# Rotating banks in the first Strassen pairs, copies on ScalarE, spread conditioning rows, and a first norm split between GpSimd and ScalarE

## The chip, the cores and the metric

The kernel runs on one NeuronCore of a Trainium2 chip, as one program with one launch. The metric is the device time of one execution in microseconds, as the median of several runs. Where a time is read inside the program it comes from one profiled execution, which has its own device time and its own span from the first to the last instruction.

## The reference, cut to what matters

One encoder layer is computed for 576 tokens: 64 frames of a running stream (group 1) and 512 frames of a new one (group 0). The matmuls keep fp32 accuracy.

```python
mod = silu(c) @ w_ada + b_ada              # 6 rows of 1024 per group: shift, scale, gate, twice
h   = rmsnorm(x, norm1_g) * (1 + sc1) + sh1
q, k, v, glu_in, g = split(h @ w_in)       # one input projection, 5632 columns
y_a = attention(q, k, v) @ w_attn_out      # window of 128 + own chunk of 64, sinks, bias
y_b = conv_module(glu_in) @ w_conv_out     # 31 taps, layernorm, swish
x   = x + gt1 * ((g_a * y_a + g_b * y_b) @ w_out)
h2  = rmsnorm(x, norm2_g) * (1 + sc2) + sh2
gate, up = split(h2 @ w_ffn_up)            # 2 x 2816 columns
x   = x + gt2 * ((silu(gate) * up) @ w_ffn_down)
y   = rmsnorm(x, final_g)
```

## The kernel before

Activations lie transposed: 128 features on the partitions, tokens along the free axis, eight such tiles for the model width. An fp32 matmul is done as three: both operands are split into a rounded high part and the rest (`hi`, `lo`), and hi·hi, hi·lo and lo·hi are summed in one PSUM bank (`mm3`, lines 320 to 322). A weight chunk comes by one DMA of 512 KB into a ring of four buffers `wraw` (`RAW`, line 241). Each half of a chunk, 128x512, is a unit: ScalarE rounds it (line 294) and GpSimd or VectorE subtracts (line 297) into rings `whi` and `wlo` of four. `split_unit` does it, one to two units ahead of the matmuls.

**First norm** (lines 434 to 575). The sum of squares gives 1/rms for all tokens, which ScalarE copies to the tile `gbr2` (line 552). For each of the eight tiles `make_t` multiplies x by scale and 1/rms on VectorE (line 436, two pieces, one per group), ScalarE adds the shift and rounds (line 472), VectorE makes the rest (line 478), and TensorE runs three passes over five weight chunks and 576 tokens (line 495). The scale of the next tile is a row of w_ada times silu(c), summed on VectorE (`ada_cols`, line 413: two instructions of 1024 elements). Four engines follow the written order here.

**Attention** (lines 870 to 1000). 32 steps, each with scores, the reduction with bias (line 893), exp on ScalarE (line 897), normalising on GpSimd (line 909), transposes and values a step later, a 24-matmul piece of the projection, and three taps of the depthwise convolution on VectorE (line 668). Before the reduction VectorE copies two sink values beside the scores (line 890). The order is as written.

**Conditioning rows** (lines 1025 to 1140). 24 further rows of w_ada are loaded and summed on VectorE: six behind the layernorm's statistics, two behind the attention projection, sixteen beside the conv projection.

**FFN up** (lines 1180 to 1390). Each of 22 pairs of a gate and an up tile is computed by seven block products of 4x12 = 12 matmuls on 288 columns (Strassen's scheme on half widths: inputs `parts_of[m, j]`, weights of product m by `pair_source`, sums and differences of the quarters g0, g1, u0, u1). Products 1 and 2 of the first eight pairs (`N_PRE`) run ahead as "early products" while VectorE still makes the other inputs; for these pairs `up` runs 6, 5, 7, 3, 4 in banks m1 (c6), s2 (c5, shared by 5 and 3) and s3 (c7, shared by 7 and 4). VectorE forms weights 5, 6, 7 and 3 (line 265) and the low parts of 6 and 7 in the first eight pairs, 5, 6 and 7 later (`LO_V`). Then VectorE adds and multiplies the products (lines 1358 to 1369), ScalarE applies silu and rounds (lines 1366, 1355), and VectorE makes the rest (line 1356).

Outside the hand-written stretches the scheduler orders each engine's instructions from a timeline of its own.

## Time and profile before

| what | value |
|---|---|
| runs | 969.54 us median of 3 (964.81 to 970.26) |
| the profiled execution | 964.45 us, span 962.7 us |
| TensorE busy | 920.9 us (96%), 6804 matmuls |
| VectorE / ScalarE / GpSimd busy | 740.8 / 459.6 / 491.8 us |
| mean granted TensorE clock | 0.985 of full |
| HBM | 111.11 MB read, 4.18 MB written, 120 GB/s |

PE is TensorE, DVE VectorE, ACT ScalarE, POOL GpSimd, SP the engine that issues all DMAs. A matmul's busy time overlaps the next one's, so a loss on PE is seen as idle time or as a wider spacing of the matmuls. An engine works through its instructions in order; one that waits holds all behind it.

### The profile page before, as it was taken

The numbers are of one execution on the slowest core, as the hardware profiler recorded it, in microseconds if no ns is written. First come the engines' busy times: TensorE is split into PE (matmuls) and PEld (weight loads), VectorE is DVE, ScalarE is ACT, GpSimd is POOL, SyncE is SP. The second block draws the span as 40 slices with busy tenths as digits, with TensorE's granted clock in tenths as the row PEclk, the third lists the DMA queues.
The fourth block names the chain that finished last, engine by engine and source line by source line (L and its number), as shares of the span: only waits on it lengthen the run. The fifth ranks groups of instructions, "written<-read, shape, count | busy, mean of one in ns | idle before, by whom it ended". The sixth has DMA issues, their size and how long they took to land.

```text
span 962.7 us, 18079 instructions
## 1 busy us (share of the span) xinstructions
PE 920.9 (96%) x6804; PEld 904.8 (94%) x6804; DVE 740.8 (77%) x1445; ACT 459.6 (48%) x1019; POOL 491.8 (51%) x459
## 2 busy tenths in 40 slices
...
GB/s 340 335 46 57 153 88 98 67 62 66 66 45 67 44 94 169 135 294 232 229 153 23 66 136 105 89 111 209 163 108 90 89 110 89 66 93 100 82 151 113
DMA packets 37917, 116.32 MB, mean 121 GB/s; under 512 B 4243, under 2 KB 9011, under 8 KB 37685
## 3 DMA queue, kind: packets, MB, share of 16 engines
...
HBM read 111.11 MB, written 4.18 MB: 120 GB/s over the span
## 4 chain that ended last, share of the span: by engine, by line
PE 68%; DVE 22%; DMA 5%; issue 2%; ACT 2%; POOL 1%; SPq 0%; DVEq 0%; ACTq 0%; POOLq 0%
PE m L320 11%; PE m L321 11%; PE m L322 11%; PE s L320 10%; PE s L322 10%; PE s L321 10%; DVE cva L668 5%; DVE dump L413 3%; DMA wraw<-w_ada_n 2%; DVE e L890 2%; DVE lsum L413 2%; DMA wraw<-w_up 1%; DVE sa L265 1%; DVE e L893 1%; DMA qa<-xT 1%
## 5 line engine op out<-in xcount | busy, mean ns | idle before, releaser
L297 POOL TENSOR_TENSOR wlo<-wraw,whi 128x512 fp32r<-128x512 f32 x216 | 295.5, 1373 | 211.6 <-ACT whi L294 175.1
L320 PE MATMUL m<-h,whi 128*128 128x320 f32 (+2 forms) x776 | 229.6, 296 | 3.3 <-ACT whi L294 3.3
L321 PE MATMUL m<-h,whi 128*128 128x320 f32 (+2 forms) x776 | 228.5, 295 | 0.0
L322 PE MATMUL m<-h,wlo 128*128 128x256 f32 (+2 forms) x776 | 228.3, 295 | 0.0
L294 ACT CAST whi<-wraw 128x512 fp32r<-128x512 f32 x248 | 149.8, 607 | 157.1 <-PE s L321 79.9
L320 PEld LDWEIGHTS m<-h,whi 128*128 128x128 f32 x776 | 146.6, 189 | 3.6 <-ACT whi L294 3.5
L322 PEld LDWEIGHTS m<-h,wlo 128*128 128x128 f32 x776 | 146.4, 189 | 0.0
L321 PEld LDWEIGHTS m<-h,whi 128*128 128x128 f32 x776 | 146.2, 188 | 0.0
L668 DVE SCALAR_TENSOR_TENSOR cva<-z,vec,cva 128x606 f32<-128x606 f32 x150 | 127.2, 848 | 1.4
L320 PE MATMUL s<-h,whi 128*128 128x288 f32 (+2 forms) x328 | 98.4, 300 | 10.1 <-DVE qa L1356 9.2
L322 PE MATMUL s<-h,wlo 128*128 128x288 f32 (+2 forms) x328 | 97.6, 298 | 0.2 <-DVE wlo L297 0.2
L321 PE MATMUL s<-h,whi 128*128 128x288 f32 (+2 forms) x328 | 97.7, 298 | 0.0
L297 POOL TENSOR_TENSOR wlo<-wx,whi 128x512 fp32r<-128x512 f32 x30 | 42.8, 1427 | 92.8 <-ACT whi L294 73.1
L320 PE MATMUL s<-qa,whi 128*128 128x288 f32 (+2 forms) x272 | 80.3, 296 | 0.4 <-ACT qa L1132 0.4
L322 PE MATMUL s<-qa,wlo 128*128 128x288 f32 (+2 forms) x272 | 80.3, 296 | 0.2 <-DVE wlo L297 0.2
L320 PE MATMUL s<-kv,whi 128*128 128x288 f32 x264 | 79.7, 302 | 0.7 <-DVE qa L1356 0.3
L321 PE MATMUL s<-qa,whi 128*128 128x288 f32 (+2 forms) x272 | 80.2, 295 | 0.0
L321 PE MATMUL s<-kv,whi 128*128 128x288 f32 x264 | 78.9, 299 | 0.0
L322 PE MATMUL s<-kv,wlo 128*128 128x288 f32 x264 | 78.6, 298 | 0.0
L320 PEld LDWEIGHTS s<-h,whi 128*128 128x128 f32 x328 | 62.6, 191 | 12.3 <-DVE qa L1356 10.8
L320 PE MATMUL m<-qa,whi 128*128 128x288 f32 (+2 forms) x240 | 71.5, 299 | 0.0
L321 PE MATMUL m<-qa,whi 128*128 128x288 f32 (+2 forms) x240 | 71.5, 298 | 0.0
...
## 6 DMA issues: line engine op xcount, KB each, us to landing
...
```

The costliest lines, as they stand in the source:

```text
L265: op(out=t, in0=x, in1=y)
L294: nc.scalar.copy(out=hi, in_=src)
L297: eng.tensor_sub(out=lo, in0=src, in1=hi.bitcast(F32))
L320: nc.tensor.matmul(out, lhsT=hi, rhs=xh, start=first, stop=False, skip_group_check=again)
L321: nc.tensor.matmul(out, lhsT=hi, rhs=xl, start=False, stop=False, skip_group_check=again)
L322: nc.tensor.matmul(out, lhsT=lo, rhs=xh, start=False, stop=last, skip_group_check=again)
L413: nc.vector.scalar_tensor_tensor(out=dumps[g], in0=wt, scalar=1.0, in1=cbt[g], op0=ALU.mult, op1=ALU.mult, accum_out=out[:, g : g + 1],)
L668: nc.vector.scalar_tensor_tensor(out=acc, in0=src, scalar=w, in1=acc, op0=ALU.mult, op1=ALU.add)
L890: nc.vector.tensor_copy(out=e[:, :, BAND], in_=nsink[:, 4 * p + 2 * u : 4 * p + 2 * u + 2])
L893: nc.vector.tensor_tensor_reduce(out=e[:, x, o:BAND], in0=sv[:, x], in1=biases[p][u][:, x, o:BAND], scale=1.0, scalar=nsink[:, c : c + 1], ...
```

## The change

Six things are changed.

1. The first eight pairs use the banks m1, s2, s3 and m0 in turn, three per pair, so that consecutive pairs start one bank apart. The later pairs keep m1, s2, s3, with m0 for products 1 and 2.
2. Weight 7 (g0 - u0) is formed on GpSimd, into the tile wx; sum 5 and weight 6 go side by side into one of two double banks in turn (for the first pair into wx and m0). VectorE makes the low parts of 6 and 5 in all pairs, GpSimd that of 7. The raw ring has five buffers.
3. The inputs of the last half are made in another order, the scaled x lies in PSUM instead of SBUF, and 1/rms in m0.
4. The sink copies go from VectorE to ScalarE.
5. The conditioning rows: none behind the layernorm's statistics, eight behind the attention projection, eight beside the conv projection (one per tile), and the last eight beside the first half of `w_out`, loaded into the raw ring (`late_row`).
6. In the first norm x is multiplied by 1/rms one or two tiles ahead, by VectorE for tiles 0 and 1 and by GpSimd for 2 to 7; ScalarE applies scale and shift in place and rounds in a further instruction; VectorE subtracts in one instruction instead of two.

```diff
-LO_V = ((6, 7), (6, 5, 7))
+LO_V = (6, 5)
 
 H2_FROM = 3
 
-ROWS, ROWS_AT = 6, 3
+ROWS_AT = 1
...
-    RAW, SPL = 4, 4
+    RAW, SPL = 5, 4
...
         if m == 6:
-            sums[c, 5] = total(nc.vector.tensor_add, u0, u1)
-            sums[c, 6] = total(nc.vector.tensor_sub, sums[c, 5], g0, "cva")
+
+            n_sum[1] += 1
+            if n_sum[1] == 1:
+                sums[c, 5] = pair_sum()
+                sums[c, 6] = bank("m0").rearrange("p (k n) -> p k n", n=P)
+            else:
+                two = bank2(("cva", "sa")[n_sum[1] % 2]).rearrange("p x (k n) -> p x k n", n=P)
+                sums[c, 5], sums[c, 6] = two[:, 0], two[:, 1]
+            nc.vector.tensor_add(out=sums[c, 5], in0=u0, in1=u1)
+            nc.vector.tensor_sub(out=sums[c, 6], in0=sums[c, 5], in1=g0)
         elif m == 7:
-            sums[c, 7] = total(nc.vector.tensor_sub, g0, u0, "sa")
+            sums[c, 7] = pair_sum()
+            nc.gpsimd.tensor_sub(out=sums[c, 7], in0=g0, in1=u0)
         elif m == 3:
-            sums[c, 3] = total(nc.vector.tensor_sub, g1, sums[c, 6])
+            sums[c, 3] = pair_sum()
+            nc.vector.tensor_sub(out=sums[c, 3], in0=g1, in1=sums[c, 6])
         return sums[c, m]
 
-    n_sum = [0]
+    n_sum = [0, 0]
 
     def pair_sum():
         n_sum[0] += 1
-        return ft([P, 4, P], f"wx{n_sum[0] % 4}")
+        return ft([P, 4, P], f"wx{n_sum[0] % 2}")
...
-        eng = nc.vector if last or (pair and pair[1] in LO_V[key[1] >= FCH[0][1]]) else nc.gpsimd
+        eng = nc.vector if last or (pair and pair[1] in LO_V) else nc.gpsimd
...
-        def make_t(k):
-            for s0, s1, g in FULL:
-                nc.vector.scalar_tensor_tensor(
-                    out=xt[k][:, s0:s1], in0=xt[k][:, s0:s1], scalar=sc_a[:, 0, k, g : g + 1],
-                    in1=rstd[:, s0:s1], op0=ALU.mult, op1=ALU.mult,
-                )
+        def norm(k):
+            (nc.gpsimd if k > 1 else nc.vector).tensor_mul(out=xt[k], in0=xt[k], in1=rstd)
...
         def make_h(k):
+
             f = SH1 + k
-            make_t(k)
             for s0, s1, g in FULL:
                 nc.scalar.activation(
-                    out=hh[k][:, s0:s1], in_=xt[k][:, s0:s1], func=AF.Identity, bias=ada[:, f, g : g + 1]
+                    out=xt[k][:, s0:s1], in_=xt[k][:, s0:s1], func=AF.Identity, scale=sc_a[:, 0, k, g : g + 1],
+                    bias=ada[:, f, g : g + 1],
                 )
+            nc.scalar.copy(out=hh[k], in_=xt[k])
             row(k + 1, 0)
             row(k + 1, 1)
-            for s0, s1, g in FULL:
-                nc.vector.scalar_tensor_tensor(
-                    out=hl[k][:, s0:s1], in0=xt[k][:, s0:s1], scalar=ada[:, f, g : g + 1],
-                    in1=hh[k][:, s0:s1].bitcast(F32), op0=ALU.add, op1=ALU.subtract,
-                )
+            nc.vector.tensor_sub(out=hl[k], in0=xt[k], in1=hh[k].bitcast(F32))
...
+            norm(0)
             shift(0)
             make_h(0)
+            norm(1)
+            norm(2)
...
+                    if n + 2 < KT:
+                        norm(n + 2)
...
-        nc.vector.tensor_copy(out=e[:, :, BAND], in_=nsink[:, 4 * p + 2 * u : 4 * p + 2 * u + 2])
+        nc.scalar.copy(out=e[:, :, BAND], in_=nsink[:, 4 * p + 2 * u : 4 * p + 2 * u + 2])
...
-        for _ in range(ROWS):
-            ada_bg()
...
-            for _ in range(2):
-                if ada_todo:
-                    ada_bg()
-        nc.vector.scalar_tensor_tensor(
-            out=sc_a[:, 1], in0=ada[:, SC2 : SC2 + 8], scalar=1.0, in1=wide(V_N2), op0=ALU.add, op1=ALU.mult
-        )
+            ada_bg()
...
-    xtags = ["wx0", "wx1", "wx2", "wx3", "gbr0", "gbr1", "gbr2", "f21"]
+    xtags = ["h12", "h13", "h14", "h15", "gbr0", "gbr1", "gbr2", "f21"]
...
+    def late_row(j, f, cbt):
+
+        t = sb([P, KT, P], "wraw", bufs=RAW).rearrange("p k n -> p (k n)")
+        nc.sync.dma_start(out=t, in_=a["w_ada_n"][j])
+        dump = sb([P, D], "lsum", BF16)
+        ada_cols(ada[:, f], t, cbt, [dump, dump])
+
     for n in range(8):
+        if n < 7:
+            late_row(*ada_todo.pop(0), cbs)
         residual(n, 0, wo(n, 0), GT1, ssqs[0])
+        if n == 6:
+            late_row(*ada_todo.pop(0), cbs)
+    add_bias(SC2)
+    nc.vector.scalar_tensor_tensor(
+        out=sc_a[:, 1], in0=ada[:, SC2 : SC2 + 8], scalar=1.0, in1=wide(V_N2), op0=ALU.add, op1=ALU.mult
...
+                early[i] = [bank(("m1", "s2", "s3")[i % 3])[:, :HB], ones_[i // 4][:, i % 4]]
...
+        add, root, spread = rstd_rows(bank("m0"), None, HB, lambda: sb([P, CA], "lsum"), False)
...
+        for j2 in (0, 2):
+            t1, t2 = {}, {}
+            for j in (j2, j2 + 1):
+                tj = bank2(("cva", "sa")[j % 2])
+                t1[j], t2[j] = tj[:, 0, :HB], tj[:, 1, :HB]
+                scale_h2(j, 1, r, t1[j])
+                scale_h2(4 + j, 1, r, x11[:, j])
+            for j in t1:
+                nc.vector.scalar_tensor_tensor(
+                    out=t1[j], in0=t1[j], scalar=sh2(j), in1=b0[:, j], op0=ALU.add, op1=ALU.subtract
+                )
+            for j in t1:
+                nc.vector.scalar_tensor_tensor(
+                    out=t2[j], in0=x11[:, j], scalar=sh2(4 + j), in1=t1[j], op0=ALU.add, op1=ALU.subtract
+                )
+                make_parts(6, j, t2[j])
+            for j in t1:
+                make_parts(5, j, t1[j])
+                nc.vector.tensor_sub(out=t1[j], in0=t2[j], in1=b0[:, j])
+                nc.vector.tensor_sub(out=t2[j], in0=b0[:, 4 + j], in1=t2[j])
+            for j in t1:
+                make_parts(7, j, t1[j])
+                make_parts(4, j, t2[j])
+                make_parts(3, j, x11[:, j], sh2(4 + j))
...
-        c1, c6, c5, c7 = (bank(t)[:, :HB] for t in ("m0", "m1", "s2", "s3"))
+        t6, t5, t7 = ("m1", "s2", "s3") if i >= N_PRE else (("m1", "s2", "s3", "m0")[(3 * i + x) % 4] for x in range(3))
+        c6, c5, c7 = (bank(t)[:, :HB] for t in (t6, t5, t7))
...
```

How the instructions move is shown at three places. First VectorE in the first eight pairs, one period of each kernel. Before, L1365, L1361, L1363 and L1369 add the products 3, 5, 7 and 4, L1358 the next pair's 6; L1354 multiplies, L1356 makes an output's low part, L265 forms weights and L297 low parts of weights; s2 is c5, s3 is c7, m1 is c6. The row that writes sa is weight 7:

```order
L1365 TENSOR_TENSOR s2_7582<-s2_7582,kv7_6628 128x288
L297 TENSOR_TENSOR wlo_7696<-sa_7693,whi_7695 128x512
L1354 TENSOR_TENSOR s2_7582<-s2_7582,t_7623 128x288
L1358 TENSOR_TENSOR kv7_6628<-m1_7690,kv7_6628 128x288
L265 TENSOR_TENSOR sa_7802<-wraw_7609,wraw_7629 128x512
L1356 TENSOR_TENSOR qa3_7492<-s2_7582,qa1_7491 128x288
L1369 TENSOR_TENSOR s3_7583<-s3_7583,kv7_6628 128x288
L1354 TENSOR_TENSOR s3_7583<-s3_7583,t_6965 128x288
L1356 TENSOR_TENSOR qa3_7492<-s3_7583,qa1_7491 128x288
L1361 TENSOR_TENSOR t_7732<-s2_7691,kv7_6628 128x288
L297 TENSOR_TENSOR wlo_7758<-cva_7755,whi_7757 128x512
L265 TENSOR_TENSOR wx0_7821<-wraw_7609,cva_7755 128x512
```

After, the same work is L1382, L1378, L1380, L1386 and L1375, L1371, L1373, L270 to L277 and L300; here c5 is m1 and c7 is s2, and the next pair has s3, m0 and m1:

```order
L1382 TENSOR_TENSOR m1_7139<-m1_7139,kv6_6629 128x288
L1375 TENSOR_TENSOR kv6_6629<-s3_7245,kv6_6629 128x288
L1371 TENSOR_TENSOR m1_7139<-m1_7139,t_7180 128x288
L1386 TENSOR_TENSOR s2_7140<-s2_7140,kv6_6629 128x288
L1373 TENSOR_TENSOR qa2_7051<-m1_7139,qa0_7050 128x288
L1371 TENSOR_TENSOR s2_7140<-s2_7140,t_6812 128x288
L270 TENSOR_TENSOR sa_7415<-wraw_7273 128x512
L1378 TENSOR_TENSOR t_7287<-m0_7246,kv6_6629 128x288
L300 TENSOR_TENSOR wlo_7312<-cva_7308,whi_7311 128x512
L271 TENSOR_TENSOR sa_7415<-sa_7415,wraw_7186 128x512
L1373 TENSOR_TENSOR qa2_7051<-s2_7140,qa0_7050 128x288
L1380 TENSOR_TENSOR t_7287<-m1_7247,t_7287 128x288
```

The row that forms weight 7 is gone, the next pair's product 5 (read by L1378) goes to a bank that the last pair has not used, and its product 7 to the bank of the last pair's product 3.

Second VectorE at the start of the first norm. Before, L413 are the two instructions of a conditioning row, L449 adds its bias, L436 makes scaled x (xt in qa0, 1/rms in gbr2):

```order
L154 TENSOR_SCALAR gbr0_251<-ident_73,rs_223 128x128
L413 SCALAR_TENSOR_TENSOR dump0_165,ada_88<-qa2_108,cb_163 128x1024
L413 SCALAR_TENSOR_TENSOR dump1_166,ada_88<-qa2_108,cb_163 128x1024
L449 TENSOR_SCALAR ada_88<-ada_88,vec_63 128x2
L436 SCALAR_TENSOR_TENSOR qa0_98<-qa0_98,sc_a_89,gbr2_170 128x64
L436 SCALAR_TENSOR_TENSOR qa0_98<-qa0_98,sc_a_89,gbr2_170 128x512
L413 SCALAR_TENSOR_TENSOR dump0_165,sc1_167<-qa3_116,cb_163 128x1024
L413 SCALAR_TENSOR_TENSOR dump1_166,sc1_167<-qa3_116,cb_163 128x1024
L478 SCALAR_TENSOR_TENSOR h8_155<-qa0_98,ada_88,h0_147 128x64
L478 SCALAR_TENSOR_TENSOR h8_155<-qa0_98,ada_88,h0_147 128x512
```

After, L438 is x times 1/rms, L416 the row, L448 its bias, L478 the low part:

```order
L154 TENSOR_SCALAR gbr0_251<-ident_73,rs_223 128x128
L438 TENSOR_TENSOR qa0_98<-qa0_98,gbr2_170 128x576
L416 SCALAR_TENSOR_TENSOR dump0_165,ada_88<-qa2_108,cb_163 128x1024
L416 SCALAR_TENSOR_TENSOR dump1_166,ada_88<-qa2_108,cb_163 128x1024
L448 TENSOR_SCALAR ada_88<-ada_88,vec_63 128x2
L416 SCALAR_TENSOR_TENSOR dump0_165,sc1_167<-qa3_116,cb_163 128x1024
L416 SCALAR_TENSOR_TENSOR dump1_166,sc1_167<-qa3_116,cb_163 128x1024
L478 TENSOR_TENSOR h8_155<-qa0_98,h0_147 128x576
L438 TENSOR_TENSOR qa0_98<-qa0_98,gbr2_170 128x576
```

The multiplication of tile 0 by 1/rms now stands ahead of the row for the shift of tile 0 (into ada), which stood ahead of everything that needs 1/rms; that of tile 1 stands behind the low part of tile 0.

Third one attention step. VectorE before, with the sink copy L890, the reduction L893 and the convolution's taps L668:

```order
L890 COPY e0_3169<-nsink_1654 128x2
L893 ISA e0_3169,nm_3167<-s2_3163,bias0_2150,nsink_1654 128x192
L893 ISA nm_3167 128x1
L893 ISA e0_3169,nm_3167<-s2_3163,bias0_2150,nsink_1654 128x192
L893 ISA nm_3167 128x1
L668 SCALAR_TENSOR_TENSOR cva_2668<-z5_663,vec_63,cva_2668 128x606 x2
L907 RECIPROCAL den_3168<-den_3168 128x2
L668 SCALAR_TENSOR_TENSOR cva_2668<-z5_663,vec_63,cva_2668 128x606
L928 TENSOR_TENSOR pl_3211<-sa_3140,ph_3210 128x768
```

ScalarE after, with the copy L892 and the exps L899 of the same step:

```order
L297 CAST whi_3151<-wraw_2644 128x512
L892 COPY e0_3163<-nsink_1648 128x2
L899 ACTIVATE e0_3163,den_3162<-e0_3163,nm_3161 128x193 x2
L929 CAST ph_3204<-sa_3134 128x768
L749 COPY gbr2_3208<-m0_3175 128x320
```

On VectorE the copy is missing after and the other rows keep their order; on ScalarE it stands just ahead of the exps that read it.

## Rows read from the trace of the kernel before

**Rows 1.** The page: busy time and share of the span.
```profile
PE 920.9 (96%) x6804; PEld 904.8 (94%) x6804; DVE 740.8 (77%) x1445; ACT 459.6 (48%) x1019; POOL 491.8 (51%) x459
```

**Rows 2.** Stretches: length, PE, PEld, DVE, ACT, POOL busy (instructions), clock, DMA, GB/s.
```profile
25.40:71.50 46.10, 41.12 (x304) 40.27 (x305) 43.28 (x68) 17.89 (x42) 27.41 (x24) 0.96 0.52 188
180.00:346.00 166.00, 162.72 (x1225) 159.75 (x1224) 149.46 (x357) 86.64 (x267) 78.40 (x110) 1.00 0.18 60
346.00:542.00 196.00, 194.54 (x1469) 193.31 (x1469) 138.93 (x292) 94.11 (x187) 98.66 (x80) 0.99 0.48 161
562.20:645.00 82.80, 69.09 (x461) 65.99 (x460) 69.52 (x123) 35.27 (x71) 35.58 (x25) 0.94 0.32 102
720.00:850.00 130.00, 129.80 (x975) 129.34 (x974) 80.71 (x153) 51.67 (x101) 60.26 (x45) 1.00 0.29 91
613.67:623.91 10.24, 8.45 (x61) 8.04 (x61) 9.46 (x16) 4.13 (x8) 4.63 (x4) 1.00 0.29 102
```

**Rows 3.** TensorE's waits: who was waited for, total us, times, longest.
```profile
PE s L320 <- DVE qa L1356: 9.5, 6, 2.1
PE m L320 <- ACT whi L294: 3.3, 1, 3.3
PE m L495 <- ACT h L472: 2.3, 1, 2.3
PE m L495 <- DVE h L478: 1.2, 1, 1.2
```

**Rows 4.** VectorE in order of time, one early pair: start, us, line, operation.
```profile
618.54 1.67 DVE L265 TENSOR_TENSOR cva<-wx,wraw 128x512 f32<-128x512 f32 x1
620.13 0.45 DVE L1365 TENSOR_TENSOR s<-s,kv 128x288 f32<-128x288 f32 x1
621.10 0.45 DVE L1354 TENSOR_TENSOR s<-s,t 128x288 f32<-128x288 f32 x1
621.83 1.67 DVE L265 TENSOR_TENSOR sa<-wraw 128x512 f32<-128x512 f32 x1
623.41 0.44 DVE L1356 TENSOR_TENSOR qa<-s,qa 128x288 fp32r<-128x288 f32 x1
```

**Rows 5.** GpSimd in order of time, the same pair.
```profile
617.99 1.67 POOL L297 TENSOR_TENSOR wlo<-wx,whi 128x512 fp32r<-128x512 f32 x1 [3.60 <-ACT whi L294]
```

**Rows 6.** VectorE's groups by shape: count, busy us, mean ns, idle before.
```profile
L890 DVE COPY e<-nsink 128x2 f32<-128x2 f32 x36 | 25.0, 693 | 0.1
L297 DVE TENSOR_TENSOR wlo<-cva,whi 128x512 fp32r<-128x512 f32 x22 | 15.2, 690 | 1.2
```

**Rows 7.** GpSimd's groups by shape.
```profile
L297 POOL TENSOR_TENSOR wlo<-wx,whi 128x512 fp32r<-128x512 f32 x30 | 42.8, 1427 | 92.8 <-ACT whi L294 73.1 <-DVE t L1358 7.5 <-DVE s L1354 6.0
L655 POOL TENSOR_TENSOR lsum<-lsum,z 128x576 f32<-128x576 f32 x6 | 8.5, 1424 | 14.0 <-ACT z L649 14.0
L297 POOL TENSOR_TENSOR z<-wraw,z 128x512 fp32r<-128x512 f32 x2 | 4.0, 1990 | 0.0
```

**Rows 8.** ScalarE's groups by shape.
```profile
L1079 ACT CAST h<-ltmp 128x576 fp32r<-128x576 f32 x8 | 5.2, 669 | 0.1
L460 ACT ACTIVATE sc_a<-sc,bsn,vec 128x2 f32<-128x2 f32 x7 | 2.7, 388 | 12.3 <-DVE dump L413 12.3
```

**Rows 9.** VectorE in order of time, the start of the first norm.
```profile
18.95 1.22 DVE L413 SCALAR_TENSOR_TENSOR dump<-qa,cb 128x1024 bf16<-128x1024 f32 x1
...
21.36 1.10 DVE L449 TENSOR_SCALAR ada<-ada,vec 128x2 f32<-128x2 f32 x1
22.38 0.93 DVE L436 SCALAR_TENSOR_TENSOR qa<-qa,sc_a,gbr 128x64 f32<-128x64 f32 x2
23.24 2.30 DVE L413 SCALAR_TENSOR_TENSOR dump<-qa,cb 128x1024 bf16<-128x1024 f32 x1
...
32.69 0.94 DVE L478 SCALAR_TENSOR_TENSOR h<-qa,ada,h 128x64 fp32r<-128x64 f32 x2
```

**Rows 10.** TensorE in order of time, the first products of the norm.
```profile
25.48 0.54 PE L495 MATMUL m<-h,whi 128*128 128x320 f32 x2
```

More of the change, by code (lines that the diff above doesn't have):

```diff
@@ L1155, in layer_kernel @@
             tg = xtags[4 * j + 2 * part : 4 * j + 2 * part + 2]
-            hold[("wo", 6 + j), 4 * part] = lambda tg=tg: tuple(ft([P, 4, P], t, F32R) for t in tg)
+            hold[("wo", 6 + j), 4 * part] = lambda tg=tg: tuple(wx(t) for t in tg)
     x1 = []
@@ L1195, in layer_kernel @@
     for j in range(4):
-        for m, i in ((1, j), (2, 4 + j), (6, 8 + j), (5, 12 + j)):
+        for m, i in ((1, j), (2, 4 + j), (6, 8 + j)):
             parts_of[m, j] = half(sb([P, NT], f"h{i}", F32R))
@@ L1256, in st_product @@
         product(out, weights(("st", i, m), ahead), lambda j: parts_of[m, j], 4, first)
+    for j in range(4):
+        parts_of[5, j] = half(sb([P, NT], f"h{12 + j}", F32R))
     early = {}
@@ L1263, in early_products @@
             if m == 1:
-                early[i] = [bank(("m0", "m1", "s2", "s3")[i % 4])[:, :HB], ones_[i // 4][:, i % 4]]
+                early[i] = [bank(("m1", "s2", "s3")[i % 3])[:, :HB], ones_[i // 4][:, i % 4]]
             bk, t = early[i]
@@ L1271, in early_products @@
                 nc.scalar.activation(out=early[i][1], in_=bk, func=AF.Silu)
-    x01, x11 = (sb([P, 4, HB], f"qa{x}") for x in (1, 3))
+    x11 = sb([P, 4, HB], "qa3")
     sh2 = lambda k: ada[:, SH2 + k, 0:1]
-    dsh = sb([P, 4], "rs", bufs=2)
-    nc.vector.tensor_sub(out=dsh, in0=ada[:, SH2 + 4 : SH2 + 8, 0], in1=ada[:, SH2 : SH2 + 4, 0])
     with tc.manual_schedule(engines={ENG.PE}):
-        add, root, spread = rstd_rows(bank("sa"), None, HB, lambda: sb([P, CA], "lsum"), False)
+        add, root, spread = rstd_rows(bank("m0"), None, HB, lambda: sb([P, CA], "lsum"), False)
         early_products(first_two[:1])
```

37 lines of the change are left out of this document (7 added, 30 removed).

## The prediction

> **What bounds the kernel now.** The page comes first: TensorE is busy for 96% of the span [rows 1]. So only its losses can be won, and the next view is a table by stretches [rows 2]. In the late pairs, 720 to 850, 975 matmuls take 129.80 us, 0.133 each, and nothing is lost. Against that:
> - In the first eight pairs, 562.2 to 645, 461 matmuls should take 61.5 us and 82.8 pass. 21.3 are lost: 13.7 as idle time (82.80 less 69.09), the rest as matmuls at the lower clock. The granted clock has a mean of 0.94 there, 1.00 in the late pairs.
> - In the attention, 180 to 346, 3.3 are lost as idle time. Most matmuls there have 256 or 320 columns; at 0.130 each 1225 take 159, which makes the loss 7.
> - In the first norm, 25.4 to 71.5, 5.0 are idle. From 346 to 542, 1.5.
>
> These four, 34.8 us, are all that the change can reach. The third view, TensorE's waits, says who was last [rows 3]: in the pairs VectorE's low part of the output, line 1356 (9.5 us in six waits), and once the rounding of a weight (3.3); in the norm the rounded h (2.3) and its low part (1.2).
>
> **The first pairs.** One pair takes 10.24 us for 60 matmuls, 8.0 us of work; VectorE is busy for 9.46 of it [rows 2]. The fourth view shows the chain [rows 4]. Product 3 ends, and L1365 reads it at 620.13, late because a weight sum stood before it for 1.67 us. L1354 follows, then the difference for weight 7 for another 1.67, then L1356 at 623.41, which ends at 623.85 and frees s2 for the next pair's product 5. Two such instructions cost 1.67 and a subtraction with one operand in PSUM 0.69 [rows 6]; the first began while GpSimd was in an instruction of 1.67 [rows 5].
>
> This row bears on a rule. The Trainium skill (SBUF — State Buffer, Who interferes with whom) says that a VectorE instruction with two SBUF inputs and a GpSimd instruction that reads SBUF exclude each other for their whole length. The trace agrees: 1.67 with two SBUF inputs, 0.69 with one.
>
> After the change weight 7 is off VectorE: 9.46 - 1.67 = 7.8 us a pair, less than the 8.0 of TensorE. GpSimd gets it: 4.63 + 1.43 [rows 7] = 6.1. And the wait itself moves: the next pair's product 5 has a fresh bank, and only its product 7 needs what L1373 (before L1356) frees, 12 matmuls or 1.6 us later. A wait of 9.5 / 6 = 1.6 us is covered by that alone. Late next is L1380, which must read product 7 before product 4 may be added in its bank. In the order of after seven VectorE instructions of 0.45 and three of 0.69 stand from L1375 on ahead of it, 5.2 us, and 0.45 of its own; in that time TensorE has at least the products 4, 5, 7 and 3 to do, 6.4. That holds by 0.7, and if the one sum left with two SBUF inputs waits as before (1.67 instead of 0.69) it is used up. So I put a pair at 8.3 us: seven pairs save 7 x 1.9 = 13.3. The bounds are 8.0 and 10.2, none to 15.4 saved.
>
> At the first pair TensorE waits 3.3 for the rounding of its first weight, whose sums had to wait for the banks cva and sa, in use for the last inputs. They now go into a free SBUF tile and m0, and no input has its two operands in SBUF any more but x11's low part. I take these 3.3. Together 16.6, say 17, of 21.3.
>
> **Attention.** 36 copies of two values cost VectorE 693 ns each, 25.0 us [rows 6], while it is busy for 149 of 166 [rows 2]. It falls to some 125 in 166, and TensorE is left as the longest. The loss is 3.3 to 7; I take 5, nearer to the second, since a step's spacing is set by VectorE throughout. Below: nothing, if another wait stands behind. ScalarE gets 36 copies; the nearest row is 0.39 for 128x2 [rows 8], 14 us on an engine idle for half the stretch. Behind the copy in its queue stand the exps of the same step, which wait for VectorE's reduction anyway; the copy is covered by that wait.
>
> **First norm.** What is gained: VectorE gives up 0.93 and 0.94 a tile [rows 9] for one subtraction of 576, 0.69 x 576 / 512 = 0.78: 15.0 less 6.2, and less 1.6 for the two tiles that it multiplies itself: 7.2 us. The idle 5.0 us of this stretch can go. What is lost: the row for the first shift ran at 18.95, while 1/rms was being made. Now the multiplication that waits for 1/rms (there by 22.4) stands before it. From 22.4: 0.78, two row instructions of 1.22 to 2.30, a bias of up to 1.10 [rows 9], so 25.6 to 28.9 instead of 23.3 for the old multiplication. Then ScalarE's two pieces as before and a rounding of 0.67 [rows 8]. The first product, 25.48 [rows 10], comes 3 to 6 us later. Against 5.0 idle this is from 2 gained to 1 lost, and the rows of the next tiles queue behind as well. GpSimd takes six multiplications of 1.42 [rows 7], 8.5 us. I take 0, from -3 to +4.
>
> A rule speaks against this part. The Trainium skill (Perfetto Trace Analysis, Optimizing Scalar/DVE Operations) warns that moving work between VectorE and GpSimd might not help because of the port that they share. By it the stage would get 8.5 - 7.2 = 1.3 us longer; the row of 2.30 beside 1.22 for the same instruction agrees that they hinder each other [rows 9].
>
> **The rest.** Conditioning rows leave the layernorm, where up to 1.5 is idle from 346 to 542, and eight go beside w_out. There VectorE has 57 us free from 346 to 542 and each row costs 2.4, so 19 are hidden. Its loads pass SP's queue between the w_out chunks: a row can hold up weights only if its buffer is late, and TensorE has four banks in hand. I take 1, from +4 to -1.5. In the 14 later pairs GpSimd gets two instructions more, 2.85 us a pair; in 720 to 850 that is 11.6 pairs, 60 to 93 us of 130, covered. The fifth raw buffer costs nothing.
>
> **Sum.** 17 + 5 + 0 + 1 = 23 from the profiled execution's 964.45: 941.5. The runs shown are 964.81, 969.54 and 970.26, their median 5.1 above it; I add half: **944 us**.
>
> **Rivals.**
> - The port takes the place of the wait. The sum with two SBUF inputs is caught in each pair for 1.0 us (1.67 less 0.69), GpSimd being in more instructions, and L1380 comes as much too late: a pair takes 9.3. 6.3 saved, 3.3 at the first pair, 3 in the attention, 3 lost in the norm. 10 gained: 957. For it: both sums of rows 4 were caught. Against it: one such sum is left of two. Chance 0.20.
> - All losses go, the clock stays up: 35 gained, 932. For it: the lower clock follows the gaps. Against it: the front of the norm gets longer. Chance 0.06.
> - The change in the pairs doesn't do what it says: L1380 stands where L1356 stood and a pair stays at 10.2. 3.3 + 5 gained: 958. It has the time of the first rival; chance 0.06.
> - GpSimd becomes the bound in the 14 later pairs. Six instructions there must fit into 84 matmuls, 11.2 us. At 1.99, the dearest row [rows 7], they take 11.9. At 2.4 a pair takes 14.4, 3.2 more, 45 in all, less 23: 989. It eats the whole gain from 2.14 on. For it: two more readers of SBUF beside VectorE. Against it: the mean is 1.43, and only one VectorE instruction a pair has two SBUF inputs. Chance 0.05.
>
> **The numbers.** The forecast has 0.63: 937 to 952. With 0.20 and 0.06 for about 957, 0.06 for 932, 0.05 for slower. A measurement of this kernel can tell 0.5%, 4.8 us. Faster than 964.7: 0.63 + 0.25 + 0.06 less a little for losses that I don't see, 0.90. Within: 0.05. Slower: 0.05. The range that leaves out two in ten is 934 to 959.
>
> **What would show it.** Right: the period of a pair at 8.0 to 8.6, VectorE at about 7.8 in it, no wait of TensorE for the output's low part, the clock at 1.00 from 562 on; in the attention less idle time of TensorE and VectorE below 130 of 166; in the norm a first product at 27 to 31 and no waits behind tile 3. Wrong: a pair above 9; the early products waiting for GpSimd; TensorE waiting for rounded w_out weights; GpSimd busy without a break in the late pairs.

## The result: 952.38 us, and the profile after

| | before | after |
|---|---|---|
| runs | 968.57 us median of 4 (964.81 to 970.26) | 952.38 us median of 4 (951.05 to 953.67) |
| ratio to before | | 0.9838, 95% interval 0.9803 to 0.9873 |
| the profiled execution | 964.45 us, span 962.7 | 953.67 us, span 951.1 |
| mean granted clock | 0.985 | 0.987 |

The change wins 16.2 us between the medians and 10.8 between the profiled executions; 25.5 and 23 were forecast. The time lies inside the range of 934 to 959, toward its slow end, and 0.4 us above the 937 to 952 that the forecast itself had.

The first view is the page's busy line for TensorE, as in [rows 1], and the table by stretches, as in [rows 2]: in each stretch the busy time of each engine with its number of instructions, the granted clock, the share of the DMA engines and GB/s.

```profile
PE 914.6 (96%) x6804; PEld 901.9 (95%) x6804; DVE 687.3 (72%) x1350; ACT 472.5 (50%) x1063; POOL 546.7 (57%) x501
```

```profile
25.40:71.50 46.10, 37.88 (x282) 37.30 (x281) 45.92 (x51) 25.19 (x52) 42.18 (x28) 0.93 0.54 190
180.00:346.00 166.00, 166.00 (x1273) 165.90 (x1272) 137.43 (x337) 95.32 (x310) 82.49 (x113) 1.00 0.19 61
346.00:542.00 196.00, 195.26 (x1485) 193.88 (x1484) 142.36 (x290) 96.35 (x188) 99.68 (x80) 1.00 0.47 163
562.20:645.00 82.80, 79.95 (x595) 78.92 (x594) 59.66 (x119) 39.63 (x78) 49.21 (x38) 1.00 0.44 140
568.23:626.27 58.04, 55.61 (x415) 54.92 (x414) 47.00 (x94) 28.42 (x57) 35.90 (x28) 1.00 0.40 124
686.00:694.00 8.00, 7.81 (x48) 7.79 (x48) 3.66 (x7) 3.52 (x7) 7.19 (x6) 0.79 0.18 66
720.00:850.00 130.00, 128.06 (x960) 127.26 (x959) 70.29 (x137) 50.71 (x98) 77.43 (x58) 1.00 0.28 89
```

Read the first number in brackets of each row. In the attention 1273 matmuls fit where 1225 did, and in the first pairs 595 for 461, at a clock of 1.00 for 0.94: these two stretches are won. (The first pairs are over at 637.4 us now, so the last 7.6 us of that row are the down projection.) In the first norm it is 282 for 304, and in the late pairs 960 for 975: these two are lost. The row 686 to 694 is new: the clock is 0.79 there, behind a wait.

TensorE's waits, as in [rows 3], name what is last now (total, times, longest; a wait for a transfer at the start, 5.6 us here and 5.0 before, is left out):

```profile
PE m L492 <- ACT h L475: 4.2, 1, 4.2
PE m L492 <- DVE h L478: 4.0, 2, 2.8
PE m L323 <- ACT whi L297: 3.9, 2, 3.5
PE s L323 <- DVE t L1378: 3.5, 6, 0.8
```

The first two are the first norm. The third is the ninth pair, the first one behind the first part of the down projection. The fourth is spread, five of its six waits over the late pairs. The wait for the output's low part, 9.5 us before, is gone.

All kernels here issue the same 6804 matmuls, nearly in the same order, so the start of the matmul with a given number can be compared. The table gives it against before, in us (minus is earlier), at the end of the first norm (number 340), ahead of the attention (1361), behind it (2381), ahead of the first pairs (3912), behind them (4593), in the ninth pair (4933) and at the last one. Each is worked out from the two traces. Kernels with the same code up to a column still differ there: after, e4, e5, e6, e7 and e8 share the first norm and lie between +3.1 and +4.8 at its end, and e10 and e11, alike up to the ninth pair, differ by 1.8 ahead of the pairs and by 2.7 behind them. What a single pair of traces shows below that size is not shown.

| kernel | norm | | attention | | pairs | ninth | end |
|---|---|---|---|---|---|---|---|
| after | +4.8 | +4.8 | -1.1 | -3.5 | -20.2 | -16.0 | -11.5 |
| e1 norm(0) behind | +1.5 | +1.5 | -4.4 | -5.4 | -22.5 | -20.3 | -14.2 |
| e2 norms on VectorE | +1.1 | +1.4 | -4.5 | -6.6 | -22.4 | -19.9 | -13.2 |
| e3 old first norm | +0.5 | +0.8 | -5.1 | -7.7 | -22.9 | -21.2 | -14.7 |
| e4 ninth pair's sums | +4.3 | +4.3 | -1.6 | -4.1 | -20.1 | -20.1 | -14.0 |
| e5 four raw buffers | +4.0 | +4.1 | -1.8 | -3.4 | -23.0 | -20.0 | -21.7 |
| e6 no rotation | +3.1 | +3.3 | -2.6 | -3.9 | -9.9 | -7.0 | +1.7 |
| e7 weight 7 on VectorE | +4.6 | +4.6 | -1.3 | -3.4 | -17.9 | -13.3 | -7.3 |
| e8 sinks on VectorE | +3.5 | +3.6 | +3.9 | +3.3 | -11.4 | -9.4 | -4.8 |
| e9 = e5 and e3 | +0.5 | +0.5 | -5.4 | -6.8 | -26.6 | -23.8 | -25.4 |
| e10 = e5, e1, e2, e4 | -1.3 | -1.0 | -6.9 | -9.0 | -27.9 | -27.9 | -23.8 |
| e11 = e5, e1, e2 | -0.7 | +0.2 | -5.7 | -7.2 | -25.2 | -22.4 | -23.2 |
| e12 = e11, rows earlier | -1.3 | -1.0 | -6.9 | -8.9 | -27.3 | -27.3 | -28.6 |

So the change won 5.9 in the attention, 2.4 from there to the pairs and 16.7 in the pairs, 25.0 together; it lost 4.8 in the first norm and 8.7 from the ninth pair on. The 5.9 of the attention is the same, within 0.1, in every kernel but e8. From there to the pairs the kernels win 0.6 to 2.6, and in the pairs those with five buffers win 14.8 to 17.1 where neither banks nor weight 7 are touched.

### The profile page after: what moved, and what is told of

Read it like the earlier page. It is cut to its first block, busy times and chain, and to the rows that moved or that the text cites. A ratio compares the mean times of both kernels' runs of the same rounds, so it can differ in the third digit from the quotient of the medians.

```text
span 951.1 us, 18123 instructions
## 1 busy us (share of the span) xinstructions
PE 914.6 (96%) x6804; PEld 901.9 (95%) x6804; DVE 687.3 (72%) x1350; ACT 472.5 (50%) x1063; POOL 546.7 (57%) x501
## 4 chain that ended last, share of the span: by engine, by line
PE 71%; DVE 14%; DMA 8%; issue 4%; ACT 1%; POOL 1%; SPq 0%; DVEq 0%; ACTq 0%; POOLq 0%
PE m L323 13%; PE m L324 12%; PE m L325 12%; PE s L323 9%; PE s L324 9%; PE s L325 9%; DVE dump L416 4%; DMA wraw<-w_ada_n 4%; DMA wraw<-w_up 3%; DVE lsum L416 2%; DMA wat<-w_ada_n 1%; PE sa L922 1%; DVE wlo L300 1%; DMA qa<-xT 1%; DVE z L1078 1%
## 5 line engine op out<-in xcount | busy, mean ns | idle before, releaser
L300 POOL TENSOR_TENSOR wlo<-wraw,whi 128x512 fp32r<-128x512 f32 x216 | 291.9, 1359 | 217.5 <-ACT whi L297 175.3
L297 ACT CAST whi<-wraw 128x512 fp32r<-128x512 f32 x248 | 149.6, 608 | 166.7 <-PE s L324 81.5
L323 PE MATMUL m<-h,whi 128*128 128x320 f32 (+2 forms) x768 | 227.0, 296 | 3.9 <-ACT whi L297 3.9
L324 PE MATMUL m<-h,whi 128*128 128x320 f32 (+2 forms) x768 | 225.9, 295 | 0.0
L325 PE MATMUL m<-h,wlo 128*128 128x256 f32 (+2 forms) x768 | 225.0, 295 | 0.2 <-DVE wlo L300 0.2
L300 POOL TENSOR_TENSOR wlo<-wx,whi 128x512 fp32r<-128x512 f32 x44 | 56.7, 1292 | 55.5 <-ACT whi L297 50.0
L324 PE MATMUL m<-qa,whi 128*128 128x288 f32 (+2 forms) x272 | 80.3, 295 | 0.0
L323 PE MATMUL m<-qa,whi 128*128 128x288 f32 (+2 forms) x272 | 80.2, 296 | 0.0
L325 PE MATMUL m<-qa,wlo 128*128 128x288 f32 (+2 forms) x272 | 79.9, 294 | 0.0
L323 PE MATMUL s<-qa,whi 128*128 128x288 f32 (+2 forms) x240 | 70.9, 296 | 0.0
L324 PE MATMUL s<-qa,whi 128*128 128x288 f32 (+2 forms) x240 | 70.9, 295 | 0.0
L325 PE MATMUL s<-qa,wlo 128*128 128x288 f32 (+2 forms) x240 | 70.4, 295 | 0.2 <-DVE wlo L300 0.2
L323 PE MATMUL s<-kv,whi 128*128 128x288 f32 x216 | 64.7, 299 | 3.6 <-DVE t L1378 3.5
L324 PE MATMUL s<-kv,whi 128*128 128x288 f32 x216 | 63.9, 296 | 0.0
```

The source lines that it names most:

```text
L297: nc.scalar.copy(out=hi, in_=src)
L300: eng.tensor_sub(out=lo, in0=src, in1=hi.bitcast(F32))
L323: nc.tensor.matmul(out, lhsT=hi, rhs=xh, start=first, stop=False, skip_group_check=again)
L324: nc.tensor.matmul(out, lhsT=hi, rhs=xl, start=False, stop=False, skip_group_check=again)
L325: nc.tensor.matmul(out, lhsT=lo, rhs=xh, start=False, stop=last, skip_group_check=again)
```

## The experiments

Times are medians, ratios are to before, whose medians beside these runs were 968.4 to 969.1 us.

### The first norm: e1, e2, e3

In the changed kernel the first product comes at 31.26 us (25.48 in [rows 10]). VectorE's timeline there (start, duration, engine, line, operation, output and inputs, and the idle time ahead with what ended it):

```profile
18.62 0.29 DVE L154 TENSOR_SCALAR gbr<-ident,rs 128x128 f32<-128x128 f32 x1
23.00 0.76 DVE L438 TENSOR_TENSOR qa<-qa,gbr 128x576 f32<-128x576 f32 x1 [4.09 <-ACT gbr L549]
23.68 2.30 DVE L416 SCALAR_TENSOR_TENSOR dump<-qa,cb 128x1024 bf16<-128x1024 f32 x1
...
30.38 2.41 DVE L416 SCALAR_TENSOR_TENSOR dump<-qa,cb 128x1024 bf16<-128x1024 f32 x1
...
32.73 1.96 DVE L478 TENSOR_TENSOR h<-qa,h 128x576 fp32r<-128x576 f32 x1
```

Two things are to be seen. VectorE stands idle for 4.09 us at the multiplication of tile 0 and has the first shift's rows behind it. And the rows, the subtraction and GpSimd's multiplications are all long. The groups of 18 to 72 us (count, busy us, mean ns) say how long. VectorE's rows before:

```profile
L413 DVE SCALAR_TENSOR_TENSOR dump<-kv,cb 128x1024 bf16<-128x1024 f32 x10 | 13.9, 1428 | 0.0
L413 DVE SCALAR_TENSOR_TENSOR dump<-qa,cb 128x1024 bf16<-128x1024 f32 x8 | 12.7, 1620 | 0.0
```

VectorE's rows after, then GpSimd's multiplications:

```profile
L416 DVE SCALAR_TENSOR_TENSOR dump<-qa,cb 128x1024 bf16<-128x1024 f32 x8 | 17.3, 2193 | 0.0
L416 DVE SCALAR_TENSOR_TENSOR dump<-kv,cb 128x1024 bf16<-128x1024 f32 x10 | 15.3, 1572 | 0.0
...
L438 POOL TENSOR_TENSOR qa<-qa,gbr 128x576 f32<-128x576 f32 x6 | 13.0, 2185 | 0.0
```

In the same groups VectorE's low parts and multiplications fall from 23.4 us (14.3 and 9.1) to 13.1 (10.4 and 2.7).

e1 moves the multiplication back, e2 takes it from GpSimd, e3 takes the old norm:

```diff
 e1
-            norm(0)
             shift(0)
+            norm(0)
 e2
-            (nc.gpsimd if k > 1 else nc.vector).tensor_mul(out=xt[k], in0=xt[k], in1=rstd)
+            nc.vector.tensor_mul(out=xt[k], in0=xt[k], in1=rstd)
 e3
 make_t, make_h and their calls as before, no norm(k)
```

> In the first norm VectorE's multiplication of tile 0 is put behind the two rows for the first shift again; the multiplications of the other tiles stay. In the trace of the changed kernel VectorE stood idle for 4.09 us ahead of that multiplication, the first product of the norm began at 35.6 us where it was at 30.5 before, and TensorE had lost 4.75 us against before by 71 us. Theory A (the order is at fault): the rows run in that idle time, the first product comes at 26 to 31, the loss by 71 us falls to 1 or less, and the time is 4 us shorter, about 948. Theory B (the port is at fault: the rows take 2.19 us on average where they took 1.62, because GpSimd multiplies beside them): the first product comes earlier, but the later ones wait, the loss by 71 us stays above 3, and the time is 951 to 953.

> All eight multiplications by 1/rms in the first norm are made by VectorE, none by GpSimd; the order of the changed kernel stays, tile 0 ahead of the first shift's rows. Theory A (order): the first product still comes at about 31 to 35 and the loss against before by 71 us stays at 4 to 6, since VectorE gets six multiplications of 0.76 more: 952 to 955. Theory B (port): the 18 rows fall from 2.19 and 1.57 us to 1.4 or less, some 8 us, against 4.6 us added, so 3 us are won: about 949.

> The first norm alone is as before (x times scale times 1/rms on VectorE in one instruction per half, no multiplication on GpSimd); all else is of the changed kernel. If the losses of the parts add up, the 4.75 us that TensorE is behind by 71 us go and the time is 947 to 948. If the later stretch would have absorbed them (another wait, at a transfer, takes their place), it stays at 951 to 953.

The first text misreads one number: it has the first product at 35.6 and 30.5 us, where the traces have 31.26 and 25.48.

Measured: 950.66 (ratio 0.981, 0.979 to 0.983), 951.82 (0.9822, 0.9795 to 0.985) and 950.21 us (0.980, 0.9772 to 0.9828). Their intervals overlap that of the change, so the times decide nothing, and e3's lies between the two that its text gives; the traces have to tell. In e1 the rows fill the idle time, and the first product comes at 25.29:

```profile
18.76 1.22 DVE L416 SCALAR_TENSOR_TENSOR dump<-qa,cb 128x1024 bf16<-128x1024 f32 x1
...
22.19 0.75 DVE L438 TENSOR_TENSOR qa<-qa,gbr 128x576 f32<-128x576 f32 x1
```

In e2 the first product still comes at 30.73, but the rows are shorter:

```profile
L416 DVE SCALAR_TENSOR_TENSOR dump<-kv,cb 128x1024 bf16<-128x1024 f32 x10 | 14.0, 1430 | 0.0
L416 DVE SCALAR_TENSOR_TENSOR dump<-qa,cb 128x1024 bf16<-128x1024 f32 x8 | 13.8, 1762 | 0.0
```

By the norm's end e1 is at +1.5 and e2 at +1.1. The six kernels with the norm as written have to be told apart first. From 18 to 24 us, where 1/rms is made, after, e4 and e7 ran at a granted clock of 0.50 to 0.55, nearly all at the lower level, and end the norm at +4.3 to +4.8; e5, e6 and e8 ran at 0.72 and end it at +3.1 to +4.0. In e6 the multiplication of tile 0 starts at 21.41 and not at 23.00, with the same instructions. Before ran at 0.72 too, so up to 1.6 of the 4.8 us go with the clock of one profiled execution and not with the change. Like against like, e1 (0.72) wins 1.6 to 2.5, e2 (0.52) 3.2 to 3.7, and both together 4.4 to 5.5 (e10 at 0.72, e11 at 0.53). So by these traces both causes are there: GpSimd's multiplications beside VectorE (the port of theory B) are the larger one, and the two nearly add up. With both mended the norm ends at -1.3 to -0.7 (e10 to e12), with the old norm at +0.5. So this part of the change costs 3 to 5 us as written, and mended it is worth 1 or 2 at most; in time e9, with the old norm, and e11, with the mended one, do not differ (940.32 and 940.66 us, below).

### The first pairs: e6, e7

```diff
 e6
-        t6, t5, t7 = ("m1", "s2", "s3") if i >= N_PRE else (("m1", "s2", "s3", "m0")[(3 * i + x) % 4] for x in range(3))
+        t6, t5, t7 = ("m1", "s2", "s3")
 e7
-            nc.gpsimd.tensor_sub(out=sums[c, 7], in0=g0, in1=u0)
+            (nc.vector if n_sum[1] <= 8 else nc.gpsimd).tensor_sub(out=sums[c, 7], in0=g0, in1=u0)
```

> In the first eight pairs products 6, 5 and 7 always use the banks m1, s2 and s3; all else of the changed kernel, with weight 7's difference still on GpSimd. Theory A (the banks carry the gain of these pairs): the wait of the next pair's early product for the output's low part comes back, 0.8 to 1.6 us a pair, a pair takes 9 to 9.6 us, and 7 to 10 of the 16.6 us won in this stretch are lost: 959 to 963. Theory B (GpSimd's taking weight 7 carries it, VectorE being short of time): a pair stays under 8.6 and the time within 2 of 952.4.

> In the first eight pairs alone the difference for weight 7 is made by VectorE again; the banks still rotate; all else of the changed kernel. Theory A (the banks carry the gain): a pair stays at 8.3 to 8.7 us and the time is 952 to 955. Theory B (VectorE's time carries it): VectorE needs its old 9.4 us a pair, a pair takes 9.2 to 9.5, and 6 to 8 us are lost: 958 to 961.

Measured: 962.11 us (0.9932, 0.9911 to 0.9953) and 957.47 (0.9885, 0.9849 to 0.9921). In the stretch itself e6 wins 6.0 where the change wins 16.7, e7 14.5; a pair takes 9.8 us in e6 and 8.6 in e7 (means of seven). So the banks carry 10.7, or 8.8 to 11.1 against the kernels with the same code there. Weight 7's move carries 2.2, and 0.3 to 2.6 against those: that it carries anything is not shown. What is left, some 4, was not tried alone. The wait for the first pair's rounded weight, 3.3 before, is gone, in e6 too. e7's median is 5.1 above the change's, of which its trace has 2.2 in this stretch and 1.9 behind it, where the edit touches nothing; why is open.

Theory A had the time of e6 (a pair a little shorter than it measured), but not its wait. TensorE's waits from 555 to 640 in e6:

```profile
PE m L323 <- ACT whi L297: 7.7, 5, 1.8
PE s L323 <- DVE qa L1373: 2.6, 4, 1.1
```

The low part (line 1373) has only 2.6. The larger one is product 6's weight, and the timelines of VectorE and then ScalarE show why it is late:

```profile
604.56 1.40 DVE L270 TENSOR_TENSOR sa<-wraw 128x512 f32<-128x512 f32 x1 [0.23 <-DMA wraw<-w_up]
605.88 0.45 DVE L1371 TENSOR_TENSOR s<-s,t 128x288 f32<-128x288 f32 x1
```

```profile
606.36 0.40 ACT L1372 CAST qa<-s 128x288 fp32r<-128x288 f32 x1 [1.97 <-DVE s L1371]
606.66 0.59 ACT L297 CAST whi<-cva 128x512 fp32r<-128x512 f32 x1
```

A sum takes 1.40, the output's product waits behind it on VectorE, ScalarE waits 1.97 for that product, and the next weight's rounding stands behind in ScalarE's queue.

### The attention: e8

```diff
-        nc.scalar.copy(out=e[:, :, BAND], in_=nsink[:, 4 * p + 2 * u : 4 * p + 2 * u + 2])
+        nc.vector.tensor_copy(out=e[:, :, BAND], in_=nsink[:, 4 * p + 2 * u : 4 * p + 2 * u + 2])
```

> The 36 copies of the sinks in the attention are VectorE's again; all else of the changed kernel. If they carry the gain of this stretch, the 5.9 us that TensorE won between 180 and 346 go: VectorE is busy for some 150 of 166 us again and the time is 957 to 959. If the gain there comes from elsewhere (the layout of the work ahead of it), TensorE keeps 3 us or more of the 5.9 and the time is 952 to 955.

Measured: 959.91 us (0.9911, 0.9881 to 0.994). All of the 5.9 us go (from +3.6 to +3.9 over the attention), and the row of the stretch is that of before [rows 2] again:

```profile
180.00:346.00 166.00, 162.76 (x1220) 160.12 (x1219) 149.29 (x355) 85.08 (x262) 79.25 (x109) 1.00 0.18 61
```

Why a copy of two values took 693 ns [rows 6] is to be seen in the trace of before: one copy on VectorE, and GpSimd's subtraction beside it.

```profile
302.09 1.22 DVE L890 COPY e<-nsink 128x2 f32<-128x2 f32 x1
```

```profile
301.99 1.30 POOL L297 TENSOR_TENSOR wlo<-wraw,whi 128x512 fp32r<-128x512 f32 x1
```

Of the 36 copies 24 began while GpSimd was in such a subtraction, and each ended 0.02 to 0.03 us behind it, after up to 1.22; the other 12 took 0.16 to 0.29. So most of what the move took from VectorE was waiting for GpSimd.

### From the ninth pair on: e4, e5

The late pairs first: VectorE's timeline in two neighbouring pairs of the changed kernel, and GpSimd's beside the second.

```profile
738.53 0.70 DVE L270 TENSOR_TENSOR sa<-wraw 128x512 f32<-128x512 f32 x1 [2.31 <-DMA wraw<-w_up]
739.14 0.45 DVE L1378 TENSOR_TENSOR t<-s,t 128x288 f32<-128x288 f32 x1
...
749.65 1.82 DVE L270 TENSOR_TENSOR cva<-wraw 128x512 f32<-128x512 f32 x1 [2.51 <-DMA wraw<-w_up]
751.39 0.44 DVE L1378 TENSOR_TENSOR t<-s,t 128x288 f32<-128x288 f32 x1
```

```profile
749.63 2.98 POOL L300 TENSOR_TENSOR wlo<-wraw,whi 128x512 fp32r<-128x512 f32 x2
```

Line 270 is the sum for weight 5 of a later pair. It stands ahead of line 1378, the addition of this pair's product 5, and waits over 2 us for its load. Where GpSimd starts an instruction in the same moment the sum then takes 1.82 and not 0.70, and product 3, which is added into the bank that line 1378 reads, waits for up to 0.8. It is not the late pairs alone: in the first pairs this sum takes 1.81 at 598.65, line 1378 follows it, and TensorE waits 0.5 at 601.0 (and 1.0 at 584.3) for that line.

At the ninth pair VectorE's timeline (first block) has the last gate row's two sums, which read cva and sa, and behind them the sums for weights 5 and 6, in cva those of a later pair, in sa the ninth pair's own; ScalarE's (second block) has the rounding of the ninth pair's weight 6:

```profile
679.72 1.22 DVE L416 SCALAR_TENSOR_TENSOR lsum<-wraw,cva 128x1024 bf16<-128x1024 f32 x1 [4.34 <-DMA wraw<-w_ada_n]
...
680.98 1.22 DVE L416 SCALAR_TENSOR_TENSOR lsum<-wraw,sa 128x1024 bf16<-128x1024 f32 x1
...
682.13 0.69 DVE L270 TENSOR_TENSOR cva<-wraw 128x512 f32<-128x512 f32 x1
...
684.07 0.69 DVE L271 TENSOR_TENSOR sa<-sa,wraw 128x512 f32<-128x512 f32 x1
```

```profile
684.84 0.59 ACT L297 CAST whi<-sa 128x512 fp32r<-128x512 f32 x1 [4.03 <-DVE sa L271]
```

```diff
 e4
+            elif n_sum[1] == 9:
+                sums[c, 5], sums[c, 6] = (ft([P, 4, P], t, F32R).bitcast(F32) for t in ("gbr0", "gbr1"))
 e5
-    RAW, SPL = 5, 4
+    RAW, SPL = 4, 4
```

> The two sums of the ninth pair (the first one after the first part of the down projection) go to two free SBUF tiles and not to the PSUM banks cva and sa, which the last gate row reads until 682.1 us. Theory A (the bank is at fault): TensorE's wait of 3.7 us at 685 for the rounded weight 6 goes, with the half clock behind it; 4 to 5.6 us less: about 947.5. Theory B (the transfer is at fault: the raw weights themselves land too late): a wait of 2 us or more stays there and the time is 950 to 953.

> Four raw weight buffers as before, not five; all else of the changed kernel. In the late pairs of the changed kernel the fifth buffer lets the sum for weight 5 of a later pair stand between the additions of products 6 and 5 on VectorE: it waits 2.1 to 2.5 us for its load to land, and where GpSimd is in an instruction then it takes 1.55 to 1.82 us and not 0.70, so that product 3 waits 0.5 to 0.95 for the addition of product 5 (seven waits, 4.5 us in all). With four buffers that sum stands behind the products' additions. Theory A (the place in VectorE's queue): the waits of product 3 for line 1378 fall from 4.5 us to under 1, TensorE wins 2 to 4 us from 690 to 930, 948 to 950. Theory B (four buffers starve TensorE of weights, as the fifth was added for): waits for rounded weights appear, above 2 us in all, and the time is 953 or more.

Measured: e4 952.16 us (0.9832, 0.9799 to 0.9864; six runs from 946.58 to 958.36), e5 942.36 (0.9737, 0.9703 to 0.9771). In e4 theory A holds where it was made: the wait falls to 0.7 and nothing is lost at the ninth pair (-20.1 and -20.1). The total doesn't follow: from there on it loses 6.1 where the change loses 4.5, by more waits for the same addition, line 1378 (1380 in e4's own count): 5.3 us in seven, six of them behind 690, where the change has 3.0 in five. In e5 theory A holds, and by more than its number. The waits for line 1378 are gone behind 690, the late pairs run at TensorE's pace, and the sum stands behind the additions:

```profile
731.75 0.46 DVE L1378 TENSOR_TENSOR t<-s,t 128x288 f32<-128x288 f32 x1 [1.85 <-PE s L325]
...
736.50 0.91 DVE L270 TENSOR_TENSOR sa<-wraw 128x512 f32<-128x512 f32 x1 [0.17 <-DMA wraw<-w_up]
```

Weights don't run short: TensorE waits 3.4 us in all for rounded ones (2.3 at the ninth pair and, as something new, 1.2 for one of w_out at 495.6) where the change waits 3.9. The gain is larger than the text had it because it isn't in the late pairs alone. Of the 10.1 us by which TensorE ends earlier than in the change, 3 are won in the first pairs, where waits of 3.8 fall to 0.8, 1.2 in the ninth and 6.1 behind it. Of these 6.1, the waits for line 1378 are 2.7; another 1.7 is what 8 us at a clock of 0.79 lose, behind the ninth pair's wait, where e5 has 1.00.

### Together: e9 to e12

```diff
 e9: four buffers, the first norm as before
 e10: four buffers, e1, e2 and e4
 e11: four buffers, e1 and e2
 e12: e11 and
             if c == 0:
-                gate_row(n)
+                for r_ in ((0, 1) if n == 0 else (n + 1,) if n < 7 else ()):
+                    gate_row(r_)
```

> Two edits of earlier runs together: four raw weight buffers, and the first norm as before. By the traces the one won 10.1 us of TensorE's time by the end (21.65 against 11.53), the other 4.3 by 71 us. Theory A (the two lie in different stretches and add up): 952.4 - 10 - 4 = 938, and TensorE is 25 us ahead of before at the end. Theory B (what the norm wins is given back at a later wait for a transfer): 941 to 943, as with four buffers alone.

> Four raw weight buffers; the sums of the ninth pair in SBUF; and the new first norm with both mendings, the multiplication of tile 0 behind the first shift's rows and all eight multiplications on VectorE. Each mending alone left TensorE 1.1 to 1.5 us behind before by 71 us. Theory A (order and port are two causes of which either hides the other): with both, by 71 us TensorE is level with before or up to 3 us ahead, and with the wait of 2.4 us for the ninth pair's weights gone the time is 934 to 937. Theory B (VectorE itself is the bound of the norm, 46 of 46 us busy): it stays 1 us behind by 71 us, and the time is 937 to 940.

> Four raw weight buffers and the first norm with both mendings (tile 0's multiplication behind the first shift's rows, all eight on VectorE), the ninth pair's sums in cva and sa again. In the run with these sums in SBUF, TensorE was 27.9 us ahead of before as the ninth pair began and lost 4.5 there, since the sum of the pair after it took the freed bank, stood ahead of weight 5's low part on VectorE and waited 3.6 us for its load. Theory A (that is the cause): without that edit the ninth pair loses 2.2 to 2.6, as in the other runs with four buffers, TensorE ends 25.5 to 27 ahead of before, and the time is 938 to 940. Theory B (the loss there is as large whatever the bank, once TensorE comes earlier): it ends 23 to 24.5 ahead and the time stays at 941 to 943.

> As the run beside it, and each gate row of the first down projection is issued one step (two products, 6.4 us) earlier: two in the first step, none in the last. Theory A (the last gate row holds the banks cva and sa until the ninth pair needs them): the wait of 2.3 us for the ninth pair's rounded weight 6 goes, and the time is 2 us under the run beside it, 936 to 938. Theory B (the rows follow one another at 6 us, each load waiting for a buffer that the row before it frees, so that none comes earlier): the last row ends as late as before, the wait stays above 1.5, and the time does not differ from the run beside it by more than 1.5.

Measured: e9 940.32 us (0.9707, 0.9672 to 0.9743), e10 941.60 (0.9718, 0.9686 to 0.9749), e11 940.66 (0.9711, 0.9693 to 0.973), e12 934.14 (0.9644, 0.9625 to 0.9663).

e9: TensorE is 25.4 us ahead at the end, as theory A has it, and the time between the two theories. e10 missed: it comes to the ninth pair 27.9 ahead and ends 23.8 ahead, with a wait of 4.0 in that pair. VectorE shows the same pattern once more. The sum of the pair after it found its bank free, stands ahead of the ninth pair's low part, and waits 3.58 for its load:

```profile
677.72 0.70 DVE L272 TENSOR_TENSOR cva<-wraw 128x512 f32<-128x512 f32 x1 [3.58 <-DMA wraw<-w_up]
678.33 1.75 DVE L302 TENSOR_TENSOR wlo<-gbr,whi 128x512 fp32r<-128x512 f32 x1
```

e11 is undecided: at the ninth pair it loses 2.8, near theory A's figure, but it came there with 25.2 instead of 27.9 and ends where theory B has it. e12 is theory A in what happens: the last gate row is over at 669.5 us, 6.9 earlier than in e11, and the sums run at once.

```profile
668.32 1.22 DVE L416 SCALAR_TENSOR_TENSOR lsum<-wraw,sa 128x1024 bf16<-128x1024 f32 x1
...
669.72 0.70 DVE L270 TENSOR_TENSOR sa<-wraw 128x512 f32<-128x512 f32 x1
```

No wait is left at the ninth pair. The time is 6.5 under e11 where 2 was expected: in the traces 2.8 of it are the ninth pair's, and 2.1 e12 has already ahead of that pair, where its code is that of e11; why is open. With 934.14 us e12 beats both kernels: 34 us under before, 18 under the change.

## Why the prediction was right, and where it was not

The time came inside the range, and the two terms that were to carry the gain came as forecast. But the sum did not: it had 23 and the traces have 11.5, since two losses, 4.8 in the first norm and 8.7 from the ninth pair on, stood in it at nothing. That the range held is owed to its width.

- **First pairs, 17 of 21.3 us: right.** 16.7 were won. The starts of line 1380 give the period:

```profile
568.23 0.44 DVE L1380 TENSOR_TENSOR t<-s,t 128x288 f32<-128x288 f32 x1
```

```profile
626.27 0.46 DVE L1380 TENSOR_TENSOR t<-m,t 128x288 f32<-128x288 f32 x1 [0.77 <-PE m L325]
```

  Seven periods in 58.04 us are 8.29, forecast 8.3; VectorE is busy for 47.0 / 7 = 6.7 of it, less than the 7.8 worked out. That the banks and not weight 7's time carry most of it is shown by e6 and e7. That the output's low part is the wait that the banks take away was only partly right: without the rotation it is 2.6 us, and the rounding behind it on ScalarE 7.7. One step was misread without harm. The next pair's product 5 gets no unused bank but the one from which the last pair's product 6 has long been read; the unused one is product 6's.
- **Attention, 5 us: right.** 5.9, and e8 shows that the copies carry it. VectorE is busy for 137 of 166 (forecast 125 to 130), since 99 of the convolution's taps, 0.85 each, now fall into the stretch and not 91. A copy takes 204 ns on ScalarE, where 388 was taken.
- **First norm, 0 us (3 lost at worst): wrong, 4.8 lost here, 3.1 to 4.8 in the six traces with this norm.** Its first product was forecast for 27 to 31 us and came at 31.26. The step that failed is the 5.0 us of idle time set against it: they did not come back. VectorE gives up more than was counted. The 15.0 us were taken from one tile's rows, 0.93 and 0.94, while the means of before are 1.14 and 1.79: 23.4 in all, of which 13.1 are left. But its rows rise from 26.6 to 32.6, eight of them from 1.62 to 2.19 each, GpSimd's six multiplications take 2.19 and not 1.42, and VectorE stands idle for 4.09 ahead of the first multiplication. The larger part is GpSimd beside VectorE (e2), the smaller the order (e1). The rule cited from the Trainium skill (Perfetto Trace Analysis, Optimizing Scalar/DVE Operations) gave the sign of this, at 1.3 us; the trace agrees with the sign and has more of it.
- **The rest, 1 us: 2.4 won up to the pairs, 0.6 to 2.6 in the other kernels.** From 346 to 542 the clock is 1.00 for 0.99. That it is the rows' move was not tried alone.
- **"The fifth raw buffer costs nothing": wrong, and the largest miss.** Against e5 TensorE ends 10.1 us later with it, 6.1 of that behind the ninth pair and some 3 in the first pairs; in time it is 10.0. The forecast had looked for a shortage of weights, and not at what a free buffer lets the scheduler pull forward.
- **The ninth pair was in no term.** Product 6 waits 3.5 us for its weight, at a granted clock of 0.79 behind it, since sums 5 and 6 are both in banks that the last gate row reads; before, sum 5 was in SBUF and ready. That it is the banks is shown by e4, where the wait falls to 0.7, and by e12, where the row ends earlier and no wait is left.
- **The rivals.** The first, a sum with two SBUF inputs caught by GpSimd in each pair, was there (1.82 against 0.70), in early and late pairs, but with line 1378 and not 1380 waiting, and at 0.4 to 1.0 in some of the pairs and not in each. GpSimd did not become the bound: 77 of 130 us. The rule of the Trainium skill (SBUF — State Buffer, Who interferes with whom) is borne out by the pair of rows 0.70 and 1.82 above.

Sum: 17 + 5 + 0 + 1 = 23 was forecast; 16.7 + 5.9 - 4.8 + 2.4 - 8.7 = 11.5 came.
